# Expert stage of a hybrid encoder block: the last gate and up steps split one raw tile at a time

## The chip, the cores and the metric

One core of a Trainium2 chip runs the whole program. The metric is the time of one execution on the device, in microseconds (us); the time of a kernel is the median over its runs. The engines are TensorE (PE; its weight loads, PEld, run beside its matmuls), VectorE (DVE), ScalarE (ACT), GpSimd (POOL) and SyncE (SP), which here only issues transfers.

## The reference

One layer of an encoder on x (1, 1024, 2048), float32: neighbourhood attention and a Hyena mixer in parallel, an output projection, and then an expert-choice mixture of experts, in which each of 16 experts picks its 128 best tokens. The change lies in the last part:

```
gate, idx = lax.top_k(jnp.swapaxes(affinity, 1, 2), cap)      # cap = 128 tokens of 1024
xg = jax.vmap(lambda hb, ib: hb[ib])(h, idx)
a  = jnp.einsum('becd,edf->becf', xg, w_gate)                 # d = 2048, f = 1024
up = jnp.einsum('becd,edf->becf', xg, w_up)
ye = jnp.einsum('becf,efd->becd', jax.nn.silu(a) * up, w_down)
ye = ye * gate[..., None].astype(ye.dtype)                    # then added back at idx
```

## The kernel before, in words

Phases 1 and 2 (attention, Hyena, output projection, router) fill the first 2.2 ms and are not touched. `phase3` (L1069 on) is the expert stage: a top-k, then for each expert `gate_up` (L1121) and `down` (L1167).

**Products in parts.** Every float32 operand is split into a high part in the type of TensorE's fast form and a low part that holds the rest (`split`, L57): ACT casts the source into the high part (L60), DVE subtracts to get the low part (L61). A product is then hi x hi, lo x hi and hi x lo, three matmuls (`products`, L1107, through `mm`, L68), each with its own weight load. The 128 tokens of an expert, transposed, are the stationary operand (xh, xl), weights are the moving one, 512 columns per matmul, and sums gather in PSUM banks of 512 columns (tile name pa).

**Weights.** `load_expert` (L945) puts 1 MB of weights into a raw tile (128 x 2048, tile name w) on SP's queue; a ring of 18 raw tiles holds them, and each call of `raw` lets one more load follow. In an expert come eight pairs (two rows k of gate, the same two of up) and then eight tiles of down. Row k means 128 of the 2048 inputs. In the first expert the last pair's two raw tiles lie in buffers (el0, el1) that later hold the activation y and its transposed parts.

**Split tiles.** wh3 and wl3 (`parts`, L1104) have 1024 columns and four buffers each. In the first six pairs of `gate_up`, and in `down`, `half` splits one half of a raw tile, one row k, with one cast and one subtraction of 1024 columns; six matmuls use it, 512 columns for each of two banks. An expert has four banks for gate and up: ps[j, n], j = 0 gate, 1 up, n the column half.

**The last four rows k (12 to 15).** They run by column halves, so that bank pair n = 0 is done while n = 1 still runs, and the activation of the first half can begin. The four raw tiles are all fetched first. For each n and each of the four rows i, one split tile takes 512 columns of gate and 512 of up, from two raw tiles, with two casts and two subtractions of 512 columns:

```
w = [raw() for j in range(4)]
for n in range(2):
    for i in range(4):
        wh, wl = parts()
        for j in range(2):
            sl = slice(j * 512, j * 512 + 512)
            c = i % 2 * FF + n * 512
            self.split(wh[:, sl], wl[:, sl], w[i // 2 * 2 + j][:, c:c + 512])
        if n == 1 and i == 2:
            turn(0)
        k = KD - 4 + i
        products([ps[0, n], ps[1, n]], xh[:, k], xl[:, k], wh, wl, False, i == 3)
    act(n)
```

`act(n)` (L1134) is Silu of gate's bank on ACT (L1136) and its product with up's bank on DVE (L1137). `turn(n)` transposes that half on PE and splits it. `turn(0)` stands ahead of the seventh split tile's products, `turn(1)` in `down`.

**Order.** PE's order is the program's (`manual_schedule` for PE alone, around the expert loop). ACT, DVE, POOL and SP get theirs when the program is built: a scheduler runs a model of the chip and gives each engine, as it comes free, the earliest instruction of the program that is ready in that model. On the chip each engine then takes its instructions in that fixed order, with semaphore waits.

Of the kernel before, what the change touches and what calls it, by code (L numbers as in the profile page):

```python
# [20 lines left out]
KD = D // P  # L21
# [4 lines left out]
FF = 1024  # L26
# [11 lines left out]
class Block:  # L38
# [1030 lines left out]
    def phase3(self, ctx):  # L1069
        tc, nc, a = self.tc, self.nc, self.a  # L1070
        self.topk()
        pa = ctx.enter_context(tc.tile_pool(name="pa", bufs=1, space=PSUM, reuse_waits="tile"))
        pt_ = ctx.enter_context(tc.tile_pool(name="pt3", bufs=2, space=PSUM, reuse_waits="tile"))

        ex = ctx.enter_context(tc.tile_pool(name="ex", bufs=1, reuse_waits="tile"))
        self.ring(ctx, "ewb", 2, side="right")
        self.ring(ctx, "ewc", 8)
        el = self.el = ctx.enter_context(tc.tile_pool(name="el", bufs=1, reuse_waits="tile"))
        self.ring(ctx, "ewd", 5)
        xh = el.tile([P, KD, P], R, name="xh", bufs=1)  # L1080
        xl = el.tile([P, KD, P], R, name="xl", bufs=1)

        def bank():
            return pa.tile([P, 512], F32, name="pa", bufs=6)

        def gather(e):
            if e == NE:
                return
            xg = ex.tile([P, D + 16], F32, name="xg", bufs=1)
            nc.gpsimd.indirect_dma_start(out=xg, out_offset=None, in_=self.xg[:, :],  # L1090
                                         in_offset=bass.IndirectOffsetOnAxis(ap=self.idx[:, e:e + 1], axis=0))
            return xg

        def load():
            ahead = self.EW + max(min(self.used, KD - self.EX) + self.EX, self.used)
            while self.loaded < min(ahead, NE * self.NW):
                self.load_expert()

        def raw():
            load()  # L1100
            self.used += 1
            return self.eraw.pop(0)

        def parts():  # L1104
            return (el.tile([P, FF], R, name="wh3", bufs=4), el.tile([P, FF], R, name="wl3", bufs=4))

        def products(out, hi, lo, wh, wl, start, stop):  # L1107

            parts_ = [(o, slice(i * 512, i * 512 + 512)) for i, o in enumerate(out)]
            for o, sl in parts_:  # L1110
                self.mm(o, hi, wh[:, sl], start, False)
                self.mm(o, lo, wh[:, sl], False, False)
            for o, sl in parts_:
                self.mm(o, hi, wl[:, sl], False, stop)

        def half(w, i):
            wh, wl = parts()
            self.split(wh, wl, w[:, i * FF:i * FF + FF])
            return wh, wl

        def gate_up(e):  # L1121


            xg = self.xg3
            rs = ex.tile([P, 16], F32, name="rs", bufs=1)
            nc.scalar.copy(rs[:, 0:1], xg[:, D:D + 1])
            ps = {}
            for n in range(2):
                for j in range(2):
                    ps[j, n] = bank()  # L1130
            y = el.tile([P, 2 * FF], F32, name="el0", bufs=1)
            h3 = el.tile([P, 2, FF // P, P], R, name="el1", bufs=1)

            def act(n):  # L1134
                s = y[:, n * 512:n * 512 + 512]
                nc.scalar.activation(s, ps[0, n], AF.Silu, scale=rs[:, 0:1])  # L1136
                nc.vector.scalar_tensor_tensor(s, ps[1, n], rs[:, 0:1], s, op0=ALU.mult, op1=ALU.mult)  # L1137

            def turn(n):
                self.turned(pt_, h3[:, 0], h3[:, 1], y, n)  # L1140

            for kk in range(KD // 2 - 2):
                if kk == 2:
                    self.xg3 = gather(e + 1)
                for j in range(2):
                    w = raw() if kk or e else None
                    for i in range(2):
                        wh, wl = half(w, i) if w is not None else ready.pop(0)
                        k = 2 * kk + i
                        products([ps[j, 0], ps[j, 1]], xh[:, k], xl[:, k], wh, wl, k == 0, False)  # L1150

            w = [raw() for j in range(4)]
            for n in range(2):
                for i in range(4):
                    wh, wl = parts()
                    for j in range(2):
                        sl = slice(j * 512, j * 512 + 512)
                        c = i % 2 * FF + n * 512
                        self.split(wh[:, sl], wl[:, sl], w[i // 2 * 2 + j][:, c:c + 512])
                    if n == 1 and i == 2:  # L1160
                        turn(0)
                    k = KD - 4 + i
                    products([ps[0, n], ps[1, n]], xh[:, k], xl[:, k], wh, wl, False, i == 3)
                act(n)
            return h3, y, lambda: turn(1)

        def down(e, h):  # L1167
            h3, y, rest = h
            ps = [bank() for n in range(4)]
            for k in range(FF // P):  # L1170
                w = raw()
                for c in range(2):
                    wh, wl = half(w, c)
                    products(ps[2 * c:2 * c + 2], h3[:, 0, k], h3[:, 1, k], wh, wl, k == 0, k == FF // P - 1)
                if k == 1:
                    rest()
                elif 3 <= k < 7 and self.xg3 is not None:
                    self.turned(pt_, xh, xl, self.xg3, k - 3, 2)
            for n in range(4):
                nc.scalar.activation(y[:, n * 512:n * 512 + 512], ps[n], AF.Copy, scale=self.gate[:, e:e + 1])  # L1180
            nc.gpsimd.indirect_dma_start(out=a["out"],
                                         out_offset=bass.IndirectOffsetOnAxis(ap=self.idx[:, e:e + 1], axis=0),
                                         in_=y, in_offset=None, compute_op=ALU.add)

        self.xg3 = gather(0)
        ready = []
        for j in range(2):
            w = raw()
            ready += [half(w, i) for i in range(2 - j)]
        ready.append(None)  # L1190
        with tc.manual_schedule(engines={mybir.EngineType.PE}):
            for kg in range(4):
                self.turned(pt_, xh, xl, self.xg3, kg, 2)
            ready[3] = half(w, 1)
            for e in range(NE):
                down(e, gate_up(e))
# [96 lines left out]
```

## Time and profile before

| | |
|---|---|
| median of three runs | 3328.8 us (3327.78 to 3339.44) |
| the profiled execution | 3332.12 us, its span 3330.3 us |
| mean granted TensorE clock | 0.986 of full |
| PE, DVE, ACT busy over the span | 96%, 70%, 55% |
| expert stage | about 2211 to 3330 us of the span |

The page gives busy shares of each engine, over the whole span and in 40 slices of 83 us; the stage of the change is slices 28 to 39. A row of the timeline is one instruction or a run of equal ones: start, length, engine, line, what it writes and reads, how many, and in brackets how long the engine had been idle and which engine's work ended that. "wl<-w,wh" is a subtraction that writes a low part from a raw tile and its high part.

### The profile page before, as it was taken

Reading aid. Unit: us, or ns where it says so; the run is one execution under the profiler, and the core shown is the slowest. Engines: PE = TensorE matmul, PEld = TensorE weight load, DVE = VectorE, ACT = ScalarE, POOL = GpSimd, SP = SyncE. Lnnn points to the kernel's source line nnn. Section 1 sums busy time; section 2 is a strip of 40 time slices with the busy share of each in tenths; the row PEclk is TensorE's granted clock in tenths of the full one; section 3 lists DMA queues with packets and bytes.
Section 4 is the critical chain, followed back from the end, with each engine's and each line's share of the span. In section 5 each row is a group of like instructions: output and inputs, shape, how many; then the busy total and the mean of one; then the engine's idle time right before and its main releaser. Section 6 shows DMA issues by size and latency. Waiting matters only on the chain.

```text
span 3330.3 us, 47541 instructions
## 1 busy us (share of the span) xinstructions
PE 3205.7 (96%) x17232; PEld 2790.5 (84%) x17232; DVE 2332.9 (70%) x3626; ACT 1842.3 (55%) x2956; POOL 77.7 (2%) x200
## 2 busy tenths in 40 slices
PE   8999999999999999999998999849999999999998
PEld 8899999997888888889987887648888888887886
DVE  5677776764566666667654332389999999898997
ACT  5455555543333333334453332338888888888886
POOL 0000000000000000000000000000000000000000
PEclk9999999999999999999999999979999999999999
DMA  7654555556565556565566564379999999999993
GB/s 247 199 165 163 165 178 189 170 162 208 192 202 196 184 192 194 186 205 167 173 212 216 170 231 143 132 311 358 401 390 402 402 396 394 380 393 400 393 397 117
DMA packets 286572, 830.71 MB, mean 249 GB/s; under 512 B 26341, under 2 KB 105360, under 8 KB 229761
## 3 DMA queue, kind: packets, MB, share of 16 engines
q1 hardware_dynamic: 280544, 791.12, 65.1%
q0 software_dynamic: 5648, 36.49, 4.3%
q8 instruction: 136, 2.23, 0.3%
q14 instruction: 100, 0.81, 0.1%
q10 hardware_dynamic: 144, 0.07, 0.0%
HBM read 751.71 MB, written 75.60 MB: 248 GB/s over the span
## 4 chain that ended last, share of the span: by engine, by line
PE 87%; DMA 5%; DVE 3%; issue 2%; ACT 2%; SPq 0%; POOLq 0%; POOL 0%; ACTq 0%; DVEq 0%
PE pj L68 30%; PE pa L68 29%; PE o L68 8%; PE c L68 6%; PE f L68 4%; PE a L68 3%; PE ct L79 2%; DMA w<-in_w_out_dram 2%; PE tp L1204 1%; ACT wh L60 1%; PE a L79 1%; PE ft L79 1%; DMA x<-in_x_dram 1%; PE l L68 1%; DMA hl<-lo_d 1%
## 5 line engine op out<-in xcount | busy, mean ns | idle before, releaser
L60 ACT CAST wh<-w 128x1024 fp32r<-128x1024 f32 (+3 forms) x1368 | 1067.6, 795 | 743.1 <-PE pj L68 383.6
L61 DVE TENSOR_TENSOR wl<-w,wh 128x1024 fp32r<-128x1024 f32 (+3 forms) x1368 | 1210.8, 904 | 327.4 <-ACT wh L60 278.5
L68 PE MATMUL pa<-wh,xh 128*128 128x512 f32 x1024 | 401.7, 392 | 8.4 <-ACT wh L60 8.4
L68 PE MATMUL pa<-wh,xl 128*128 128x512 f32 x1024 | 399.0, 390 | 0.0
L68 PE MATMUL o<-wh,m 128*128 128x512 f32 x1008 | 330.2, 400 | 1.0 <-ACT wh L60 1.0
L68 PE MATMUL pj<-wh,hh 128*128 128x384 f32 x896 | 315.8, 352 | 2.9 <-ACT wh L60 2.9
L68 PE MATMUL pa<-wl,xh 128*128 128x512 f32 x1024 | 318.0, 391 | 0.0
L68 PE MATMUL pj<-hh,wh 128*128 128x512 f32 x768 | 314.7, 410 | 0.0
L68 PE MATMUL pj<-hl,wh 128*128 128x512 f32 x768 | 304.4, 396 | 6.8 <-DMA hl<-lo_d 6.7
L68 PE MATMUL pj<-wl,hh 128*128 128x384 f32 x896 | 304.8, 340 | 0.0
L68 PE MATMUL pj<-wh,hl 128*128 128x384 f32 x896 | 304.2, 340 | 0.0
L68 PE MATMUL pj<-hh,wl 128*128 128x512 f32 x768 | 302.6, 394 | 0.0
L68 PE MATMUL pa<-wh,el 128*128 128x512 f32 x1024 | 283.9, 399 | 0.0
L68 PEld LDWEIGHTS pa<-wh,xh 128*128 128x128 f32 x1024 | 192.4, 188 | 51.3 <-ACT wh L60 12.7
L68 PEld LDWEIGHTS pa<-wl,xh 128*128 128x128 f32 x1024 | 192.3, 188 | 43.4 <-DVE wl L61 3.7
L68 PEld LDWEIGHTS pa<-wh,xl 128*128 128x128 f32 x1024 | 192.6, 188 | 39.1
L68 PEld LDWEIGHTS o<-wh,m 128*128 128x128 f32 x1008 | 189.7, 190 | 39.0 <-ACT wh L60 1.9
L68 PEld LDWEIGHTS pa<-wh,el 128*128 128x128 f32 x1024 | 187.4, 189 | 35.8
L68 PE MATMUL o<-wl,m 128*128 128x512 f32 x504 | 198.2, 394 | 0.7 <-DVE wl L61 0.7
L68 PEld LDWEIGHTS pj<-wh,hh 128*128 128x128 f32 x896 | 169.7, 189 | 8.7 <-ACT wh L60 3.2
L68 PEld LDWEIGHTS pj<-hh,wl 128*128 128x128 f32 x768 | 144.4, 188 | 34.4
L68 PEld LDWEIGHTS pj<-wl,hh 128*128 128x128 f32 x896 | 169.8, 190 | 3.0 <-DVE raw L732 1.6
(304 smaller groups left out, 5274.0 us busy)
## 6 DMA issues: line engine op xcount, KB each, us to landing
hl<-lo_d SPq DMA_DIRECT2D x608, 256.0 KB, 3.0
w<-in_w_down_dram SPq DMA_DIRECT2D x128, 1024.0 KB, 11.7
w<-in_w_up_dram SPq DMA_DIRECT2D x127, 1024.0 KB, 9.3
w<-in_w_gate_dram SPq DMA_DIRECT2D x127, 1024.0 KB, 8.3
w<-in_w_at_dram SPq DMA_DIRECT2D x120, 384.0 KB, 3.4
w<-in_w_out_dram SPq DMA_DIRECT2D x64, 512.0 KB, 4.1
w<-in_w_hy_dram SPq DMA_DIRECT2D x96, 256.0 KB, 3.5
Hd<-H SPq DMA_DIRECT2D x32, 513.0 KB, 4.2
```

The lines of the kernel that those rows point to most:

```text
L60: nc.scalar.copy(hi, src)
L61: nc.vector.tensor_tensor(lo, src, hi.bitcast(F32), op=ALU.subtract)
L68: self.nc.tensor.matmul(out, w, x, start=start, stop=stop)
L79: self.nc.tensor.transpose(pt[:, i * P:(i + 1) * P], b, self.ident)
L1204: self.nc.tensor.transpose(pt[:, i * P:(i + 1) * P], src[:, c:c + (P - 1) * step + 1:step], self.ident)
```

## The change

Each of the eight split tiles now takes one column half n of both rows k of one raw tile: split tile i reads w[i] alone, gate for even i, up for odd i, by one cast and one subtraction of 2 x 512 columns. Its six matmuls all go to one bank, ps[j, n]. So per half the order is gate of rows 12 and 13, up of rows 12 and 13, gate of rows 14 and 15, up of rows 14 and 15, and gate's bank is complete after the third tile, up's after the fourth. Loads, matmul count, buffers, `act` and `turn` stay as they are.

```
             w = [raw() for j in range(4)]
             for n in range(2):
                 for i in range(4):
+                    kk, j = KD // 2 - 2 + i // 2, i % 2
                     wh, wl = parts()
-                    for j in range(2):
-                        sl = slice(j * 512, j * 512 + 512)
-                        c = i % 2 * FF + n * 512
-                        self.split(wh[:, sl], wl[:, sl], w[i // 2 * 2 + j][:, c:c + 512])
+                    self.split(wh.rearrange("p (i f) -> p i f", i=2), wl.rearrange("p (i f) -> p i f", i=2),
+                               w[i].rearrange("p (i f) -> p i f", i=2)[:, :, n * 512:n * 512 + 512])
                     if n == 1 and i == 2:
                         turn(0)
-                    k = KD - 4 + i
-                    products([ps[0, n], ps[1, n]], xh[:, k], xl[:, k], wh, wl, False, i == 3)
+                    for m in range(2):
+                        k, sl = 2 * kk + m, slice(m * 512, m * 512 + 512)
+                        self.mm(ps[j, n], xh[:, k], wh[:, sl], False, False)
+                        self.mm(ps[j, n], xl[:, k], wh[:, sl], False, False)
+                    for m in range(2):
+                        k, sl = 2 * kk + m, slice(m * 512, m * 512 + 512)
+                        self.mm(ps[j, n], xh[:, k], wl[:, sl], False, k == KD - 1)
                 act(n)
```

## Rows read from the trace of the kernel before

**Rows 1.** The page: busy time, busy tenths in 40 slices, one load's row.

```profile
PE 3205.7 (96%) x17232; PEld 2790.5 (84%) x17232; DVE 2332.9 (70%) x3626; ACT 1842.3 (55%) x2956; POOL 77.7 (2%) x200
...
PE   8999999999999999999998999849999999999998
...
DVE  5677776764566666667654332389999999898997
ACT  5455555543333333334453332338888888888886
...
w<-in_w_up_dram SPq DMA_DIRECT2D x127, 1024.0 KB, 9.3
```

**Rows 2.** Windows of one expert each, experts 3, 6, 7 and 8: length, busy time.

```profile
2347.50:2415.87 68.37, 68.37 (x314) 56.80 (x313) 63.04 (x65) 56.99 (x70) 3.08 (x2) 1.00 1.01 396
...
2552.60:2620.97 68.37, 68.37 (x314) 56.80 (x313) 63.04 (x65) 56.99 (x70) 2.80 (x2) 1.00 1.01 403
2620.97:2690.69 69.72, 68.88 (x313) 56.61 (x313) 63.03 (x65) 56.86 (x70) 3.11 (x2) 1.00 1.01 395
2690.69:2760.42 69.73, 68.89 (x314) 56.65 (x313) 63.04 (x65) 56.92 (x70) 3.11 (x2) 1.00 1.00 392
```

**Rows 3.** Waits of the expert stage: who waited for whom, total, times, longest.

```profile
ACT wh L60 <- PE pa L68: 176.6, 568, 0.7
...
PEld pa L68 <- ACT wh L60: 12.7, 10, 1.3
...
PE pa L68 <- ACT wh L60: 8.4, 10, 0.8
PEld pa L68 <- DVE wl L61: 3.7, 10, 0.4
...
PE tp L1204 <- DVE el L1137: 0.9, 1, 0.9
```

**Rows 4.** Timeline of ACT, last gate and up steps of the sixth expert.

```profile
2582.16 1.06 ACT L60 CAST wh<-w 128x1024 fp32r<-128x1024 f32 x1 [0.31 <-PE pa L68]
2583.52 1.15 ACT L60 CAST wh<-w 128x512 fp32r<-128x512 f32 x2 [0.30 <-PE pa L68]
2584.88 1.14 ACT L60 CAST wh<-w 128x512 fp32r<-128x512 f32 x2 [0.21 <-PE pa L68]
2586.24 1.14 ACT L60 CAST wh<-w 128x512 fp32r<-128x512 f32 x2 [0.22 <-PE pa L68]
...
2593.04 0.62 ACT L60 CAST wh<-w 128x512 fp32r<-128x512 f32 x1 [0.22 <-PE pa L68]
2593.57 0.68 ACT L1136 ACTIVATE el<-pa,rs 128x512 f32<-128x512 f32 x1
```

**Rows 5.** Timeline of ACT, the same steps of the seventh expert.

```profile
2651.89 0.63 ACT L60 CAST wh<-w 128x512 fp32r<-128x512 f32 x1 [0.30 <-PE pa L68]
2653.25 2.19 ACT L60 CAST wh<-w 128x512 fp32r<-128x512 f32 x4 [0.73 <-PE pa L68]
2655.97 0.62 ACT L60 CAST wh<-w 128x512 fp32r<-128x512 f32 x1 [0.53 <-PE pa L68]
2657.33 1.14 ACT L60 CAST wh<-w 128x512 fp32r<-128x512 f32 x2 [0.74 <-DVE wl L61]
2658.69 2.18 ACT L60 CAST wh<-w 128x512 fp32r<-128x512 f32 x4 [0.22 <-PE pa L68]
2661.33 1.14 ACT L60 CAST wh<-w 128x512 fp32r<-128x512 f32 x2 [0.46 <-DVE wl L61]
2662.76 0.62 ACT L60 CAST wh<-w 128x512 fp32r<-128x512 f32 x1 [0.29 <-PE pa L68]
2663.28 0.69 ACT L1136 ACTIVATE el<-pa,rs 128x512 f32<-128x512 f32 x1
2663.86 2.67 ACT L60 CAST wh<-w 128x512 fp32r<-128x512 f32 x3
```

**Rows 6.** Timeline of PE and its weight loads in the seventh expert's stall.

```profile
2658.94 0.39 PE L68 MATMUL pa<-wh,xh 128*128 128x512 f32 x1
...
2659.17 0.39 PE L68 MATMUL pa<-wh,xl 128*128 128x512 f32 x1
...
2660.40 0.19 PEld L68 LDWEIGHTS pa<-wh,xh 128*128 128x128 f32 x1 [1.26 <-ACT wh L60]
2660.40 0.50 PE L68 MATMUL pa<-wh,xh 128*128 128x512 f32 x1 [0.84 <-ACT wh L60]
...
2661.29 0.19 PEld L68 LDWEIGHTS pa<-wl,xh 128*128 128x128 f32 x1 [0.37 <-DVE wl L61]
```

**Rows 7.** Timeline of SP's queue: the seventh expert's last gate and up loads.

```profile
2609.95 0.33 SPq L953 DMA_DIRECT2D w<-in_w_gate_dram  x1
2612.66 0.33 SPq L953 DMA_DIRECT2D w<-in_w_up_dram  x1
```

**Rows 8.** Casts and subtractions of the expert stage by shape: busy, mean ns.

```profile
L61 DVE TENSOR_TENSOR wl<-w,wh 128x1024 fp32r<-128x1024 f32 x625 | 750.9, 1224 | 77.4 <-ACT wh L60 40.9
L60 ACT CAST wh<-w 128x1024 fp32r<-128x1024 f32 x624 | 650.8, 1055 | 149.5 <-PE pa L68 144.9
...
L61 DVE TENSOR_TENSOR wl<-w,wh 128x512 fp32r<-128x512 f32 x248 | 160.1, 688 | 18.8 <-ACT wh L60 13.9
L60 ACT CAST wh<-w 128x512 fp32r<-128x512 f32 x248 | 142.1, 618 | 42.8 <-PE pa L68 30.8 <-DVE wl L61 12.0
```

**Rows 9.** Timeline of the last down step: ACT's copy waits for a bank.

```profile
3316.88 0.62 PE L68 MATMUL pa<-wl,el 128*128 128x512 f32 x2
...
3317.31 2.62 ACT L1180 ACTIVATE el<-pa,gate 128x512 f32<-128x512 f32 x4 [3.25 <-PE pa L68]
```

## The prediction

> **What bounds the kernel now.** The page's busy line comes first: TensorE (PE) works 96% of the span, VectorE (DVE) 70%, ScalarE (ACT) 55%; in the expert stage, slices 28 to 39, DVE and ACT show 8 or 9 tenths too, so there all three are close [rows 1]. So the stage is read by itself, expert by expert. From the last step of one "down" to that of the next, experts 2 to 6 take 68.37 us, all of it PE busy, and the last ten take 69.73 us [rows 2]: 1.36 us more, ten times, 13.6 us in all. The waits of the stage say on whom PE waits: ACT's casts, ten times (12.7 us on the weight-load side, 8.4 us of it also seen by the matmuls), and VectorE's subtraction ten times, 3.7 us; nothing on a weight transfer [rows 3]. So PE sets the pace, except for one stall in each of the last ten experts.
>
> Where that stall lies: in the part that the change rewrites. Call the four raw tiles of the last steps W0 to W3 (gate and up of rows 12 and 13, gate and up of rows 14 and 15) and the eight split tiles T0 to T7, four for each column half n. Before, every T is cast in two pieces, gate then up. In an early expert ACT makes them two by two, one pair per buffer that PE frees, every 1.36 us, and the first half's activation comes after the fifteenth piece [rows 4]. In a late expert the groups are 1, 4, 1, 2, 4, 2, 1 [rows 5]. PE frees buffers at the same 1.36 us beat (T0's at 2651.89, T1's at 2653.25, then T2, T3, T4, T5 at 2654.61, 2655.97, 2657.33, 2658.69). PE begins T2 at 2658.94, does two matmuls with its gate half and stands until 2660.40 [rows 6]: the up half of T2 is the third cast of the group begun at 2658.69, the eleventh of the stretch, where program order would have it sixth. Five pieces stand before it: one of T3, and both of T4 and of T5. All ten casts ahead of it read W0, W1, W2; it is the first that needs W3.
>
> So the order was fixed when the program was built, by a scheduler that believed W3 late (only PE's order is written by hand). On the chip W3 is not late: its load was issued at 2612.66 [rows 7] and such loads land in 9.3 us [rows 1], over 30 us before T2 is begun. The scheduler's wrong clock, not data, costs the 1.36 us.
>
> **The change, part by part.** Bytes, loads, matmuls, weight loads and buffers stay the same in number: 48 matmuls in the rewritten steps of an expert before and after, each with its own weight load [rows 1]; six in a row now go to one bank instead of pairs alternating between two, and two into one bank already follow each other after 0.23 us (2658.94, 2659.17) [rows 6], so 0 us.
>
> Fewer instructions: 8 casts and 8 subtractions of 1024 columns replace 16 and 16 of 512 in each expert. On ACT that is 2 x 618 - 1055 = 181 ns per tile, on DVE 2 x 688 - 1224 = 152 ns [rows 8]; over 128 tiles 23 and 19 us of engine time. What hides it: in the early experts the dearer pairs already kept PE waiting for nothing, with ACT idle 0.22 us before each [rows 4], so this is worth 0 us on the path there. The source is now two runs of 512 with a gap; no row has that form. Bounds: at best the 1055 ns and 1224 ns of the long form, at worst the two short ones; even the worst fits the 1.36 us beat, so 0 at both ends.
>
> Earlier release: W0 and W2 are given up one tile sooner, so two loads of an expert are issued about 1.4 us sooner on SP's queue; since weights lie 30 us ahead, 0 us. In the first expert W2 lies in the buffer that the activation writes; freeing it earlier shortens a 0.9 us wait of the transposes for DVE [rows 3]. Gain 0 to 0.9 us; I take 0.
>
> The order on ACT, the term that counts. With one cast per T nothing can be torn apart as in [rows 5], and the 1.36 us goes. But the change also moves dependencies. Gate's bank gets its last sum from T2 (W2) instead of T3, so the first half's activation (Silu) needs T0 and T2 alone; up's needs T3 (W3). If W3 is late in the scheduler's clock, then T3's cast is not ready, while Silu becomes ready as soon as PE has done T2. Silu takes no split buffer. T4 and T5 do, and [rows 5] show no tile begun ahead of an earlier tile, so I expect those not to pass. The queue of ACT then reads T0, T1, T2, Silu, T3. On the chip, where ACT takes its queue in order, Silu waits for PE's last matmul of T2, and T3's cast is queued behind it, with T4 to T7; the lead of three tiles is gone.
>
> Its price: the last matmul of a tile starts 0.23 us before the next tile could and lasts 0.39 us, and ACT starts 0.04 us after such an end (3316.88 + 0.39 = 3317.27, ACT at 3317.31) [rows 9]: +0.20 us. Silu holds ACT 0.58 us (2663.28 to 2663.86) [rows 5], T3's cast 1.055 us [rows 8], PE starts 0.05 us later: PE begins T3 1.88 us late. Its subtraction takes 1.22 us [rows 8], its four matmuls with the high part only 0.91 us: 0.35 us more with the hand-over, as the 0.37 us in [rows 6]. Then DVE, with no lead, also has the 0.75 us product of up and Silu to fit in before the transposes: two tiles leave 2 x (1.36 - 1.23) = 0.26 us of slack and its lead must cover the rest; I take 0.2 us, bounds 0 and 0.75. Sum 2.4 us per expert (2.2 to 3.0) in place of 1.36: +1.0 us (+0.9 to +1.6). Ten experts: +10 us (+9 to +16).
>
> Perfetto Trace Analysis, section Optimizing Scalar/DVE Operations, in the Trainium skill, says that where these engines are not saturated but cause bubbles elsewhere, breaking instructions up may let work finish sooner, which speaks against merging. The trace agrees as far as it goes: the stall of rows 6 ended on a 0.62 us half cast. By that rule halves would let PE start T3 some 0.43 us sooner, and the sum would be +6 us instead of +10; the rows are followed.
>
> Against its own time: the profiled execution spans 3330.3 us and took 3332.1; +10 gives 3342.1. That execution lay 3.3 us above the median, 3328.8, of the three runs; I forecast for the median: 3328.8 + 10 = **3338.8 us**. About 0.5%, 16.6 us, is what a measurement of this kernel can tell from no change.
>
> **The rivals.**
> Clean order: T3's cast stays ahead of Silu. It needs W3, in the scheduler's clock, to land before PE is done with T2. All that the order of [rows 5] proves is that W3 came after the buffer of T5, that is after T1 was done; T2 ends one beat of 1.36 us later, so the margin can be small. For it: the early experts, where everything is in order. Against: the pattern is the same ten times, a scheduler short of weights for good; W1 also came after T1's gate piece. Then the whole stall goes: 3328.8 - 13.6 = 3315.2 us, with the first expert's 0.9 us 3314.3.
>
> Both activations pass: in the second half too, Silu goes ahead of T7's cast, if T7's buffer (that of T3) is free late in the scheduler's clock. A second full drain costs another 2.2 us per expert: 10 x 3.2 = +32, 3361 us, slower by 1%. It decides only if T3's buffer is free after T6's products, three beats after its own; [rows 5] show pieces of T6 flowing on after W3. Unlikely.
>
> No effect: tiles pass T3 as pieces did, or the gapped form costs more than bounded; about 1.4 us per expert remains and the time stays at 3329 us. T4 and T5 ahead of T3 would be this case.
>
> **How the numbers follow.** Silu ahead of T3: 0.70, with its own range 3333 to 3346 us. Clean order 0.18, no effect 0.07, both 0.05. The range must leave out no more than 2 in 10: 0.70 without its tails does not suffice, so it goes down to the clean case, 3314 to 3346 us. Faster by over 0.5% (below 3312.2) needs the clean case and some microseconds of luck: 0.05. Slower by over 0.5% (above 3345.4): both activations 0.05, and the top of the likeliest case, 0.10: 0.15. Same: 0.80.
>
> **What would show it.** In the late experts of the new trace: 8 casts of 1024; between the third and the fourth an activation that idles for PE, then PE waiting some 1.9 us for ACT and 0.35 us for DVE, and 70.7 us per expert. The clean case shows 68.4 us in all experts and the activation after the seventh or eighth cast. The forecast falls if late experts lose their wait altogether, or if the early experts change at all.

## The result, and the profile after

Over six runs each, the changed kernel takes 3351.07 us (3349.84 to 3361.02) and the kernel before 3329.77 us (3327.37 to 3339.44): ratio 1.0068, 95% interval 1.0054 to 1.0083. That is 18 to 28 us slower, 5 us above the top of the forecast range, with the forecast sign of the likeliest case but about twice its size.

The profiled execution took 3349.84 us, its span is 3348.1 us. From the start of the second expert to the end of the span it is 3348.1 - 2277.80 = 1070.3 us, against 3330.3 - 2279.14 = 1051.2 us before: **+19.1 us** in the stage of the change. (What lies ahead of it varies between executions: in the profiled ones here the second expert begins at 2275.12 to 2291.79 us, so the stage's own length is used below.)

First the page of the changed kernel: busy time and the granted clock in 40 slices.

```profile
PE 3215.6 (96%) x17232; PEld 2794.7 (83%) x17232; DVE 2313.9 (69%) x3498; ACT 1827.8 (55%) x2828; POOL 78.0 (2%) x200
...
PEclk9999999999999999999999999879999999999999
```

The same 17232 matmuls, 128 casts and 128 subtractions fewer, and engines hardly less busy than in [rows 1]. Nothing on this page tells where 19 us went; the stage has to be read expert by expert. The windows of experts 6, 7 and 8 of the changed kernel (length, then busy time and count of PE, PEld, DVE, ACT, POOL, then granted clock, DMA share, GB/s):

```profile
2550.95:2619.23 68.28, 68.28 (x313) 56.76 (x313) 62.53 (x57) 56.29 (x62) 2.79 (x2) 1.00 1.01 404
2619.23:2691.55 72.32, 70.54 (x314) 57.69 (x313) 61.51 (x57) 55.89 (x62) 3.10 (x2) 0.98 0.97 376
2691.55:2762.48 70.93, 69.16 (x313) 56.45 (x313) 61.32 (x57) 55.74 (x62) 3.15 (x2) 1.00 0.97 379
```

Beside [rows 2], the sixth expert is almost as it was (68.28 for 68.37 us). The late ones, 69.73 us before, now alternate: experts 7 to 15 take 72.32, 70.93, 72.37, 70.92, 72.36, 70.92, 72.35, 70.92 and 72.34 us. The clock column differs with them: 0.98 in the longer ones, 1.00 in the shorter.

The waits of the expert stage, changed kernel:

```profile
ACT el L1136 <- PE pa L68: 48.4, 10, 4.8
PEld pa L68 <- ACT wh L60: 21.3, 10, 2.1
PE pa L68 <- ACT wh L60: 17.1, 10, 1.7
PEld pa L68 <- DVE wl L61: 8.7, 25, 0.5
```

In [rows 3] PE waited for ACT ten times and 8.4 us; it is still ten times, for twice as long. The first line is new among the long waits: ten times, 4.8 us each, ACT's activation (Silu) waits for PE. ACT's timeline in the seventh expert shows where:

```profile
2652.85 1.06 ACT L60 CAST wh<-w 128x1024 fp32r<-128x1024 f32 x1 [0.30 <-PE pa L68]
2658.75 0.69 ACT L1136 ACTIVATE el<-pa,rs 128x512 f32<-128x512 f32 x1 [4.84 <-PE pa L68]
2659.33 4.82 ACT L60 CAST wh<-w 128x1024 fp32r<-128x1024 f32 x5
```

T2's cast, then Silu, which stands 4.84 us for the end of PE's products of T2, then T3's cast and the four behind it: T0, T1, T2, Silu, T3, the queue of the forecast. PE and its weight loads, same expert:

```profile
2660.42 0.50 PE L68 MATMUL pa<-wh,xh 128*128 128x512 f32 x1 [1.71 <-ACT wh L60]
...
2662.56 0.63 PE L68 MATMUL pa<-wh,xh 128*128 128x512 f32 x1
2662.98 0.63 PE L68 MATMUL pa<-wh,xl 128*128 128x512 f32 x1
...
2660.42 0.19 PEld L68 LDWEIGHTS pa<-wh,xh 128*128 128x128 f32 x1 [2.13 <-ACT wh L60]
2661.68 0.36 PEld L68 LDWEIGHTS pa<-wl,xh 128*128 128x128 f32 x2 [0.50 <-DVE wl L61]
```

PE stands 1.71 us (the stand before, [rows 6], was 0.84 us). And about 1.5 us after it has begun again, its matmuls start 0.42 us apart (2662.56, 2662.98) where they start 0.23 us apart in [rows 6]. Single microseconds around it show why; seventh expert first, the corresponding stretch of the eighth last:

```profile
2661.00:2662.00 1.00, 0.93 (x4) 0.50 (x3) 1.00 (x2) 1.00 (x2) 0.00 (x0) 0.93 0.19 66
2662.00:2663.00 1.00, 1.00 (x4) 0.71 (x4) 0.96 (x2) 1.00 (x2) 0.00 (x0) 0.50 0.00 0
...
2664.00:2665.00 1.00, 1.00 (x4) 0.81 (x3) 1.00 (x2) 0.65 (x2) 0.00 (x0) 0.50 0.73 229
...
2666.00:2667.00 1.00, 1.00 (x9) 0.82 (x7) 0.95 (x1) 0.68 (x1) 0.00 (x0) 1.00 1.04 393
...
2734.30:2735.30 1.00, 1.00 (x6) 0.79 (x5) 1.00 (x2) 1.00 (x2) 0.00 (x0) 1.00 0.02 8
```

The granted clock is 0.50, the lower of TensorE's two levels (1.2 for 2.4 GHz), from just before 2662 to after 2665, and full again at 2666. PE had stood 1.71 us and had then worked for 1.5 us. In the eighth expert, after an equal stand, it stays 1.00. So the 19 us has two parts: 70.93 - 69.73 = 1.20 us in each of ten experts, 12.0 us; and 72.35 - 70.92 = 1.43 us in each of the five where the clock falls, 7.2 us. Together 19.2 us; the five experts ahead of them (2 to 6) are shorter by 0.4 us in all, which leaves 18.8 of the 19.1 us measured.

### The profile page after: what moved, and what is told of

It is laid out like the page before. It is cut to its first block, busy times and chain, and to the rows that moved or that the text cites. A ratio compares the mean times of both kernels' runs of the same rounds, so it can differ in the third digit from the quotient of the medians.

```text
span 3348.1 us, 47152 instructions
## 1 busy us (share of the span) xinstructions
PE 3215.6 (96%) x17232; PEld 2794.7 (83%) x17232; DVE 2313.9 (69%) x3498; ACT 1827.8 (55%) x2828; POOL 78.0 (2%) x200
## 4 chain that ended last, share of the span: by engine, by line
PE 86%; DMA 5%; DVE 4%; issue 3%; ACT 2%; SPq 0%; POOLq 0%; POOL 0%; ACTq 0%; DVEq 0%
PE pj L68 29%; PE pa L68 29%; PE o L68 8%; PE c L68 5%; PE f L68 4%; PE a L68 3%; PE ct L79 2%; DMA w<-in_w_out_dram 2%; PE tp L1208 1%; DVE wl L61 1%; PE a L79 1%; ACT wh L60 1%; PE ft L79 1%; DMA x<-in_x_dram 1%; PE l L68 1%
## 5 line engine op out<-in xcount | busy, mean ns | idle before, releaser
L60 ACT CAST wh<-w 128x1024 fp32r<-128x1024 f32 (+2 forms) x1244 | 1052.1, 856 | 725.4 <-PE pj L68 379.9
L61 DVE TENSOR_TENSOR wl<-w,wh 128x1024 fp32r<-128x1024 f32 (+2 forms) x1244 | 1193.0, 979 | 355.9 <-ACT wh L60 307.6
```

The costliest lines, as they stand in the source:

```text
L60: nc.scalar.copy(hi, src)
L61: nc.vector.tensor_tensor(lo, src, hi.bitcast(F32), op=ALU.subtract)
```

## The experiments

The theory to test: **order on ACT** costs the first part, because Silu, put ahead of T3's cast, empties PE's lead of split tiles; **TensorE's stand** costs the second, because the clock falls after it. The rivals: the merged tiles themselves (six matmuls in a row to one bank, sources with a gap) are what costs; or the fall of the clock has another cause than the stand. In several kernels an instruction is chained behind an earlier one of its engine when the program is built (`tc.issue_after`), which sets its place in that engine's queue. `e1` to `e4` were timed together, beside 30 runs of the kernel before (median 3334.81 us in that session; the totals expected for them count from 3330 us, so the savings are compared below, by the ratios). From e5 on each kernel ran once, so the stage and its experts say more than the total.

**e1: Silu of the first half, with its product on DVE, behind the sixth cast (T5).**

```
-        nc.scalar.copy(hi, src)
+        self.cast = nc.scalar.copy(hi, src).ins
...
+                    if n == 1 and i == 1:
+                        with tc.issue_after(self.cast):
+                            act(0)
...
-                act(n)
+            act(1)
```

> The changed kernel, with the first half's Silu queued on ACT behind the cast of the sixth split tile (T5) instead of ahead of the fourth (T3); the same instructions otherwise. Theory A, the place of Silu in ACT's queue is the whole loss: the ten late experts fall from 70.9 and 72.35 us to 68.3, PE waits for no cast, the granted clock stays at 1.00, and the time is 3330 - 10 x 1.4 - 1 = 3315 us (3313 to 3317), 1.1% under the changed kernel. Rival B, the new form of the tile costs (a source with a gap, six matmuls into one bank): the late experts stay above 70 us and the time at 3340 us or more.

Measured: 3323.71 us, ratio to before 0.9962 (0.9948 to 0.9976). ACT's timeline around Silu in the seventh expert, and that expert's window:

```profile
2665.57 1.06 ACT L60 CAST wh<-w 128x1024 fp32r<-128x1024 f32 x1 [0.30 <-PE pa L68]
2667.38 0.69 ACT L1136 ACTIVATE el<-pa,rs 128x512 f32<-128x512 f32 x1 [0.76 <-PE pa L68]
...
2627.87:2696.21 68.34, 68.34 (x313) 56.67 (x313) 61.64 (x57) 55.91 (x62) 3.10 (x2) 1.00 1.01 400
```

Silu still waits for PE, but 0.76 us for 4.84, and three tiles lie split ahead of it, so PE never waits for ACT. All late experts take 68.34 to 68.37 us at a full clock, and the kernel saves 12.7 us (8 to 17) on the kernel before, of 15 expected. The same merged tiles, the same instructions, and both parts of the loss are gone: it is the order, and nothing in the merging.

**e2: Silu directly behind T3's cast.**

```
-                act(n)
+                with tc.issue_after(self.cast):
+                    act(n)
```

> The changed kernel, with each Silu queued on ACT just behind the cast of the tile traced before it (T3 for the first half), so ahead of T4's. Theory A: a smaller dose of the same. Silu still waits for PE to end T2, but T3 is cast by then, and PE has 1.36 us of it to do: PE reaches T4 1.36 us after T2, its high part comes 0.20 + 0.58 + 1.05 + 0.05 = 1.88 us after, its low part 0.3 us late: 0.8 us per late expert (0.5 to 1.1), 69.1 us each, no fall of the clock (PE idles only half a microsecond), 3315 + 8 = 3323 us (3320 to 3327). Rival: any Silu that waits for PE in the middle of the casts costs the same wherever it stands: 71 us per late expert, 3343 us and more.

Measured: 3338.95 us, ratio 1.0003 (0.9988 to 1.0017); late experts 69.76 to 69.83 us, a full clock. Weight loads that waited, seventh expert:

```profile
2670.21 0.19 PEld L68 LDWEIGHTS pa<-wh,xh 128*128 128x128 f32 x1 [0.78 <-ACT wh L60]
2671.47 0.30 PEld L68 LDWEIGHTS pa<-wl,xh 128*128 128x128 f32 x2 [0.49 <-DVE wl L61]
2673.26 0.30 PEld L68 LDWEIGHTS pa<-wl,xh 128*128 128x128 f32 x2 [0.57 <-DVE wl L61]
```

One place later in the queue shortens the wait for ACT from 2.13 to 0.78 us, by the beat of 1.36 us. But the lead is still one tile only, and VectorE, without lead, is late twice, the second time because its product (L1137) stands ahead of the subtraction. Hence 0.7 us more per late expert than expected, and nothing saved on the kernel before, where 7 us was expected. The wait of Silu itself counts the beats: 4.84 us behind T2, 3.48 behind T3, 0.76 behind T5 (e1).

**e3: up before gate in each pair, nothing prescribed.** The bank that Silu reads is then completed by the fourth tile.

```
-                    kk, j = KD // 2 - 2 + i // 2, i % 2
+                    kk, j = KD // 2 - 2 + i // 2, 1 - i % 2
...
-                               w[i].rearrange("p (i f) -> p i f", i=2)[:, :, n * 512:n * 512 + 512])
+                               w[i // 2 * 2 + j].rearrange("p (i f) -> p i f", i=2)[:, :, n * 512:n * 512 + 512])
```

> The changed kernel with up's tile ahead of gate's in each pair of the last steps (T0 up, T1 gate, T2 up, T3 gate), so that Silu needs the last tile T3 and nothing is ready before W3 is taken; no order is prescribed. Theory A: Silu then stands behind T4's cast or later by the scheduler's own choice, late experts at 68.3 us, 3315 us (3313 to 3317). Rival B, the tile's form: as the changed kernel, 3340 us or more. Rival C, the scheduler finds another bad place (the down tiles, the product on DVE): 69 us or more per late expert, 3322 us or more.

Measured: 3325.07 us, ratio 0.9976 (0.9963 to 0.9989). The seventh expert's window:

```profile
2629.55:2697.83 68.28, 68.28 (x313) 56.76 (x313) 61.57 (x57) 56.13 (x62) 3.10 (x2) 1.00 1.01 398
```

The scheduler, left alone, now puts Silu behind the seventh cast: a dependency that completes later does what the chain did in e1. What it gains here it pays in part elsewhere: early experts take 68.47 to 68.52 us, and in the first expert the transposes wait 2.2 us for DVE's product, 0.8 us in the changed kernel. By the ratio it saves 8 us (4 to 12), of 15 expected.

**e4: the kernel before, each piece's cast chained behind the piece before.**

```
+            prev = None
...
-                        self.split(wh[:, sl], wl[:, sl], w[i // 2 * 2 + j][:, c:c + 512])
+                        if prev is None:
+                            self.split(wh[:, sl], wl[:, sl], w[i // 2 * 2 + j][:, c:c + 512])
+                        else:
+                            with tc.issue_after(prev):
+                                self.split(wh[:, sl], wl[:, sl], w[i // 2 * 2 + j][:, c:c + 512])
+                        prev = self.cast
```

> The kernel before, with each piece's cast of the last steps queued on ACT behind the piece before it in the program; same instructions, same tiles. Theory A: the 1.36 us of its ten late experts is order alone, so they fall from 69.73 to 68.4 us, at most 68.8 since the Silu may still take a place ahead of a later piece: 3330 - 13.6 = 3316 us (3315 to 3321), as good as the merged form. Rival D, the sixteen short casts and subtractions themselves fill ACT and DVE in the late experts: 69.7 us stays and 3330 us.

Measured: 3322.24 us, ratio 0.9966 (0.9956 to 0.9976). ACT in the seventh expert, and its window:

```profile
2657.26 1.14 ACT L60 CAST wh<-w 128x512 fp32r<-128x512 f32 x2 [0.21 <-PE pa L68]
2658.61 1.14 ACT L60 CAST wh<-w 128x512 fp32r<-128x512 f32 x2 [0.22 <-PE pa L68]
...
2623.62:2692.10 68.48, 68.48 (x313) 56.68 (x313) 61.58 (x65) 56.30 (x70) 3.11 (x2) 1.00 1.00 391
```

The pairs of [rows 4] return in place of the 1, 4, 1, 2, 4 of [rows 5], and with them 68.48 us. The stall before was order alone, without any merging. By the ratio that saves 11 us (8 to 15), of 14 expected. Merged tiles in good order (e1) are some 0.1 us per late expert better still, 1 us over ten, which the two ratios don't tell apart.

**e5: Silu forced ahead of T3's cast in experts 2 to 16.** Does the price need a late expert?

```
+                    first = n == 0 and i == 3 and e > 0
+                    held = None
+                    if first:
+                        held = silu(0)
+                    with tc.issue_after(held) if held is not None else ExitStack():
+                        self.split(...)
```

> The changed kernel, with T3's cast queued behind Silu in experts 2 to 16, so the bad order also in the five experts that had a good one. Theory A: experts 2 to 6 go from 68.3 us to what the late ones take, 70.9 us where the clock holds and 72.35 us where it falls, so each of the fifteen has ACT's Silu idle some 4.8 us for PE and PE idle 1.7 to 2.1 us for ACT; the run is 5 x 2.6 to 5 x 4 us longer than the changed kernel, 3365 to 3370 us. Rival: the late experts lose for another reason (weights, the other engines), and the early ones stay under 69.5 us.

Measured: 3376.84 us (before 3333.16), 7 us above the expected range; but the second expert began 9.6 us later than in the changed kernel's profile, and from there on it takes 3375.1 - 2287.4 = 1087.7 us, 17.4 us more than the changed kernel, within the 13 to 20 expected. Windows of four successive early experts:

```profile
2287.40:2359.76 72.36, 70.58 (x313) 57.70 (x313) 61.42 (x57) 55.91 (x62) 3.11 (x2) 0.98 0.96 373
2359.76:2430.71 70.95, 69.18 (x313) 56.45 (x313) 61.37 (x57) 55.72 (x62) 3.11 (x2) 1.00 0.97 377
2430.71:2503.08 72.37, 70.60 (x313) 57.69 (x313) 61.43 (x57) 55.94 (x62) 3.19 (x2) 0.98 0.98 385
2503.08:2575.37 72.29, 70.52 (x314) 57.69 (x313) 61.49 (x57) 55.92 (x62) 3.15 (x2) 0.98 0.96 375
```

Experts that took 68.28 us now take the late ones' 70.95 or 72.37 us: put Silu there and both losses follow, wherever the expert stands. The clock falls after 8 of the 15 stands (experts 2, 4, 5, 7, 9, 11, 13 and 15), in 4 and 5 in succession, so a fall doesn't shield the next stand.

**e6: the stand filled.** Seven matmuls of 512 columns, into a bank that nobody reads, between T2's and T3's products of the ten late experts; they are added work that doesn't enter the output.

```
+                    if n == 0 and i == 2 and e >= 6:
+                        fill = pt_.tile([P, 512], F32, name="tp3")
+                        for r in range(7):
+                            self.mm(fill, xh[:, 0], wh[:, :512], True, True)
```

> The changed kernel, with seven matmuls of 512 columns, into a bank that nobody reads, between PE's products of T2 and T3 in the ten late experts: PE works through the time in which it stood for ACT. Theory E, the second loss comes of PE standing still: the granted clock stays at 1.00 everywhere, no expert takes 72.35 us, all ten take 70.9 us (70.7 to 71.3), about 7 us less than the changed kernel. Rival F, the clock falls in every second expert for another reason (the length of an expert, DVE, transfers): the 0.98 windows and the 1.4 us stay in five of ten.

Measured: 3341.02 us, from the second expert on 1064.1 us, 6.2 less than the changed kernel (about 7 expected); the late experts take 70.96 to 70.98 us. The seventh's window and the stage's waits for ACT:

```profile
2616.96:2687.92 70.96, 70.76 (x320) 57.76 (x320) 61.34 (x57) 55.72 (x62) 3.11 (x2) 1.00 0.97 380
...
ACT el L1136 <- PE pa L68: 48.4, 10, 4.8
PEld pa L68 <- ACT wh L60: 5.5, 10, 0.6
```

Silu and T3's cast are as late as ever (4.8 us, ten times), so the first part stays to the 0.03 us. But PE is kept busy for most of the wait, the clock is 1.00 in all ten, and the second part is gone. So, with e7 below, the fall follows the stand of PE, not the order or the work behind it. One rival is left: the added matmuls could have changed the distance between the stands instead, which by itself made falls rarer in e9 and e10 below. Against it: stands that come 70.9 to 71.0 us after one without a fall, the distance of the late experts here, were followed by a fall each time in the changed kernel (four of four), in e5 (six of six) and in e11 (four of four).

**e7: the stand lengthened.** Silu four times in a row ahead of T3's cast (the same output, three times more than needed) in the ten late experts: as in e5, for `e >= 6`, with `held = silu(0)` four times.

> The changed kernel, with the Silu of the first half run four times in a row ahead of T3's cast in the ten late experts (the same result written again): PE stands 3 x 0.58 = 1.74 us longer. Theory E: more standing still makes the clock fall in more of the ten experts, eight to ten instead of five; an expert takes 70.9 + 1.74 = 72.6 us, plus 1.4 us where it falls, 74.0. Rival F: the fall keeps to every second expert, five of ten, 72.6 and 74.0 in turn.

Measured: 3391.38 us. The seventh expert's window, a later one's, a microsecond of the ninth expert's stand, and the waits:

```profile
2628.79:2702.71 73.92, 70.05 (x313) 57.77 (x313) 61.75 (x57) 58.00 (x65) 3.10 (x2) 0.98 0.94 367
3152.11:3227.20 75.09, 71.22 (x313) 58.57 (x313) 61.95 (x57) 58.03 (x65) 3.13 (x2) 0.95 0.94 364
...
2819.00:2820.00 1.00, 0.00 (x0) 0.00 (x0) 0.00 (x0) 1.00 (x2) 0.00 (x0) 0.50 0.18 74
...
PE pa L68 <- ACT wh L60: 38.7, 10, 3.9
```

With stands of 3.9 us the clock falls in all ten late experts, not in every second; in nine of them it falls while PE still stands, as in the ninth (0.50 with PE at rest). Periods are 73.92 to 75.1 us, mostly a microsecond above the 74.0 expected, for two reasons: four Silu in a row lengthen the stand by 2.16 us, not 1.74, and in eight of the ten the clock stays low for 6.8 us instead of 3.4 (0.95 over the expert, for 0.98).

**e8: T3 split in two pieces of 512 behind Silu, ten late experts.** As e5 for `e >= 6`, and within the chained block:

```
+                        if first:
+                            for m in range(2):
+                                sl = slice(m * 512, m * 512 + 512)
+                                self.split(wh[:, sl], wl[:, sl], w[i][:, m * FF:m * FF + 512])
```

> The changed kernel, with T3 alone, of the ten late experts, split in two pieces of 512 behind Silu: PE can start on the first piece. PE stands 1.055 - 0.62 = 0.43 us less, and the low part's wait shrinks with it: 70.5 us per expert (70.4 to 70.7) instead of 70.9 where the clock holds. Theory E: the clock falls in fewer than five of the ten experts. Rival F: still in five. A rival on the price: what PE loses at T3 is set by DVE, which must do two subtractions of 688 ns instead of one of 1224, and 70.9 us stays.

Measured: 3355.93 us, but from the second expert on (2291.79 us here) 1062.4 us, 7.9 less than the changed kernel; late experts 70.81 to 70.87 us, no fall of the clock in any. Weight loads that waited, seventh expert, and PE's own stand:

```profile
2673.98 0.19 PEld L68 LDWEIGHTS pa<-wh,xh 128*128 128x128 f32 x1 [1.71 <-ACT wh L60]
2674.50 0.19 PEld L68 LDWEIGHTS pa<-wh,xh 128*128 128x128 f32 x1 [0.22 <-ACT wh L60]
2675.30 0.19 PEld L68 LDWEIGHTS pa<-wl,xh 128*128 128x128 f32 x1 [0.28 <-DVE wl L61]
2676.72 0.30 PEld L68 LDWEIGHTS pa<-wl,xh 128*128 128x128 f32 x2 [0.41 <-DVE wl L61]
2678.51 0.30 PEld L68 LDWEIGHTS pa<-wl,xh 128*128 128x128 f32 x2 [0.57 <-DVE wl L61]
...
2673.98 0.50 PE L68 MATMUL pa<-wh,xh 128*128 128x512 f32 x1 [1.28 <-ACT wh L60]
```

The first wait is 0.42 us shorter than in the changed kernel, as the forecast's working said of halves. But the four small waits behind it make 1.48 us, where the eighth expert of the changed kernel has three of 1.03 us in all, and most of the gain is given back: VectorE has no lead, so a cast that ends sooner mostly moves the wait to the subtraction. The rival on the price holds, and the 70.5 us expected does not come. What halves do save here is the fall of the clock: PE's own stand is 1.28 us, and the clock stays 1.00.

**e9 and e10: other distances from stand to stand.** The changed kernel with 4 or 8 matmuls added in `down`, far from the stand, into a bank that nobody reads.

```
+                if k == 2 and e >= 5:
+                    fill = pt_.tile([P, 512], F32, name="tp3")
+                    for r in range(4):
+                        self.mm(fill, h3[:, 0, 0], wh[:, :512], True, True)
```

> Changed kernel with 4 matmuls of 512 columns added in the ten late experts, into a bank that nobody reads, in the down product, far from the stand of TensorE (about 0.9 us more from stand to stand; the computation itself is unchanged). Theory G: which stands are followed by a fall of the granted clock hangs on when they come, so with another spacing it need not be every second one any more; periods 71.8 us without and 73.3 us with a fall. Rival H: a fall keeps the next expert free of one, so it stays strictly every second, 5 of 10.

> As the run with 4 added matmuls, with 8 (about 1.8 us more from stand to stand). Theory G: another pattern than every second expert, and another than with 4; periods 72.7 us without and 74.2 us with a fall. Rival H: strictly every second, 5 of 10.

Measured: 3358.22 and 3369.08 us. Of e9 the windows of experts 8 and 9, of e10 those of 11 and 12:

```profile
2695.91:2769.16 73.25, 71.48 (x317) 58.43 (x317) 61.94 (x57) 55.86 (x62) 3.11 (x2) 0.98 0.96 376
2769.16:2841.02 71.86, 70.09 (x317) 57.20 (x317) 61.88 (x57) 55.65 (x62) 3.10 (x2) 1.00 0.97 376
```

```profile
2915.73:2989.91 74.18, 72.41 (x321) 59.20 (x321) 62.05 (x57) 55.84 (x62) 2.90 (x2) 0.98 0.96 369
2989.91:3062.64 72.73, 70.96 (x321) 57.94 (x321) 61.85 (x57) 55.65 (x62) 3.11 (x2) 1.00 0.97 375
```

The seventh expert drops out of both: the longer `down` already moves Silu behind T3 (e9) or T4 (e10) there. Of the nine equal stands left, the clock falls after one in e9 (expert 8) and after two in e10 (11 and 13). The periods are those expected, strictly every second is refuted, and which stand is followed by a fall changes with the distance between them.

**e11: the changed kernel once more.**

> The changed kernel once more. Theory G: which stands are followed by a fall of the granted clock hangs on when they come, to within fractions of a microsecond, so another execution of the same program need not show the same experts (7, 9, 11, 13, 15), though all ten stands come again, 72.35 us with and 70.92 us without a fall. Rival P: the program fixes it, and the same five experts fall.

Measured: 3353.46 us. Experts 7 and 8:

```profile
2622.52:2694.81 72.29, 70.51 (x314) 57.73 (x313) 61.49 (x57) 55.98 (x62) 3.10 (x2) 0.98 0.96 379
2694.81:2765.75 70.94, 69.17 (x313) 56.45 (x313) 61.34 (x57) 55.87 (x62) 3.15 (x2) 1.00 0.97 380
```

Here the expectation of Theory G fell: although the second expert began 3.3 us later in this execution, it is again experts 7, 9, 11, 13 and 15. That speaks for a pattern set by the program and its spacing, but one repetition doesn't show it: in the seventh expert the fall came nearly as long after the stand as before (1.32 and 1.45 us), so the second execution may have met the same timing by chance. By what rule the stands are picked, these runs leave open.

## Why the prediction was wrong in size, though right on the order

**What bounds the kernel, and the cause of the old stall: right.** PE sets the pace, and the 1.36 us were an order fixed at build time: e4 removes them with that order alone. Weights had nothing to do with it on the chip; that the scheduler took W3 for late is the forecast's reading, and no run shows it.

**Fewer instructions, the gapped source, the order of matmuls over the banks: right at 0 us on the path.** Casts of 2 x 512 columns are no dearer; the stage's rows of the changed kernel by shape (busy, mean ns):

```profile
L61 DVE TENSOR_TENSOR wl<-w,wh 128x1024 fp32r<-128x1024 f32 x748 | 890.7, 1223 | 125.4 <-ACT wh L60 84.7
L60 ACT CAST wh<-w 128x1024 fp32r<-128x1024 f32 x747 | 775.1, 1054 | 176.6 <-PE pa L68 170.7 <-DVE wl L61 3.4 <-DVE xl L61 0.4
```

1054 and 1223 ns, with the gapped ones among them, as [rows 8]. DVE's busy time fell by 19.0 us as computed, but by luck, and ACT's by 14.5 us, not 23: in the sixth expert DVE's fell by 0.51 us (63.04 to 62.53) and ACT's by 0.70 us (56.99 to 56.29), 64 and 88 ns per tile for the 152 and 181 forecast, because short instructions back to back overlap (1.14 us for two casts in [rows 4], not 2 x 0.62). The rest fell in the late experts and comes of the order there: e4, with the short pieces in a good order, shows much the same for DVE (61.58 us, from 63.03). The forecast also called any change of the early experts a sign of being wrong; they got shorter by 0.09 us each, with PE busy throughout. Merging alone is not the cause, since in e6 the early experts read 68.37 us with the same merged tiles; what is, was not tried.

**The order on ACT: right, in all ten late experts.** The rivals of the same part did not occur: no clean order, and the second half's Silu is in its place (the wait of L1136 counts ten, not twenty). The clean order's price was about right, as e1 shows: 13.6 us forecast, 12.7 us (8 to 17) measured.

**The price of one drain, at a full clock: right but for some 0.2 us.** In the eighth expert, with a full clock, PE's matmuls read: T3 begun at 2732.73 instead of 2730.86, 1.87 us late (forecast 1.88); 0.46 us at its subtraction and the restart (0.35); 0.3 us behind that, most of it at DVE's later waits (0.2). The sum is 70.93 - 68.28 = 2.65 us where 2.4 (2.2 to 3.0) was forecast; times ten, 12.0 us against the old stall for 10 (9 to 16).

**The step that failed:** "PE begins T3 1.88 us late", and then "Sum 2.4 us per expert (2.2 to 3.0)". The sum takes PE to go on at the speed that it had before, and has no term for its clock. The runs put 1.43 us in its place for each fall, five falls in ten experts, 7.2 us: e6, with the same lateness of T3 and no stand, loses the first part and not this one; e7, with a longer stand, has it in one expert after the other. With this term the likeliest case would have read 3328.8 + 10 + 7.2 = 3346 us, and 3348 us with the 12.0 us measured for the other. The late experts of the kernel before couldn't show this price, since their stands of 0.84 us were followed by no fall. But ahead of the expert stage the same trace has one: PE stands 2.58 us and works on, and some 2.3 us later the clock is at 0.50:

```profile
2002.33 1.06 PE L68 MATMUL l<-wr,xt 128*128 128x16 f32 x8 [2.58 <-ACT xt L1003]
...
2005.00:2006.00 1.00, 1.00 (x4) 0.71 (x4) 0.00 (x0) 0.00 (x0) 0.00 (x0) 0.50 0.89 365
```

The forecast lengthened a stand to 1.88 us, between one that cost no clock and one that did, without asking what the clock column would do.

**The rule on breaking instructions up** (the Trainium skill, Perfetto Trace Analysis, section Optimizing Scalar/DVE Operations), weighed in the forecast, is borne out by e8 in its letter, since the first wait ends 0.42 us sooner. Apart from the falls that it spared, it was worth per expert only about 0.1 us against an unslowed expert (70.85 for 70.93), because the subtraction was late next.

**The best version** is the change with its order mended. e1 (0.9962) beats both kernels; the kernel before with its own order mended (e4, 0.9966) does as well within the measurement.

## What to carry to other kernels

Merging or regrouping instructions also moves the moment at which a consumer becomes ready, and where a scheduler fixes an in-order queue at build time, that can put the consumer ahead of the work that feeds the bottleneck: look for who now stands ahead of whom, and chain the order (or let the bank complete later, as e3) rather than hope for it. An activation that waits for TensorE belongs behind the casts that keep TensorE supplied. When a forecast lengthens a stand of TensorE, carry a second term for its clock and look at the clock column in windows of a microsecond.

## What the runs showed of the hardware that was not expected

- After stands of 1.71 us the granted clock fell to 0.50 only once PE had begun again (1.5 us after, in the seventh expert), and stayed there some 3.4 us; with stands of 3.9 us (e7) it fell, in nine of ten, during the stand. In the expert stage a fall came with stands of 1.71 us in five of ten experts (8 of 15 in e5, one of nine in e9, two of nine in e10), with each stand of 3.9 us, and never with the 0.84 us of the kernel before, the shorter stands of e2 or the 1.3 us of e8. The length of a stand alone doesn't decide: in the kernel before, ahead of the expert stage, one of 1.05 us (to 1848.79) with eight matmuls of only 16 columns behind it was followed by a fall at 1850.6.
- Equal stands have unequal consequences, and the same ones in the two executions of the changed kernel that were traced (e11). With 4 or 8 matmuls more between them, fewer falls came: a kernel can so get faster or slower by 1.43 us per stand through a change elsewhere.
